# The Delta stage of a three-layer kernel: the first head's stage 1 and substitution go ahead of the second head's projections, and keys are projected first

## The chip, the core and the metric

The kernel runs on one core of one Trainium2 chip. The metric is the device time of one execution in microseconds (us). The core has five instruction queues that matter here: TensorE (PE, with its weight loads shown as PEld), VectorE (DVE), ScalarE (ACT), GpSimd (POOL) and SyncE (SP), which issues most DMA transfers.

## What is computed

The input is one sequence of 1024 positions with 1024 channels. Three layers follow each other: an RG-LRU block, a gated delta rule block with 8 heads of 128 channels, and a hybrid layer of a convolution and an S5 state space model. The change lies in the delta rule block alone. For one head, cut to what matters:

```python
q, k, v = silu(causal_dwconv(proj, conv_w))        # width 4, per channel
q, k = l2norm(q) * DK ** -0.5, l2norm(k)
a_mat = where(strict, einsum('cd,md->cm', k * beta, k) * decay_mask, 0)
t_mat = inverse(a_mat + eye)                       # per chunk, lower triangular
w, u = t_mat @ (k * beta * exp(g)), t_mat @ (v * beta)
for each chunk:                                    # the state S goes from chunk to chunk
    v_new = u - w @ S
    o = q_dec @ S + attn @ v_new
    S = S * e_last + k_dec.T @ v_new
```

The result of a head is normalised, gated with silu(z) and projected back to 1024 channels.

## The kernel before, in words

The kernel is one Python function in which every operation is given to a scheduler in program order, and the scheduler fixes each engine's list when the program is built. Program order is the priority: among the operations whose operands are ready by the scheduler's own estimate of durations, the one given earlier is placed first, and a later one fills a gap. On the chip every engine then runs its list in that fixed order and waits, with all that stands behind, where an operand is late. A tile of a pool has a tag and a number of buffers; a new tile waits until an old one of its tag is let go.

In the Delta stage (lines 608 to 959) the sequence is cut into 8 chunks (NT) of 128 positions. The gates of all heads are computed once (lines 614 to 654) and written to a DRAM tile `gb_d`. Then each of 8 heads (NH) goes through these helpers:

- `dense(h)` (line 677) projects q, k and v. On even heads it loads and splits three weight blocks, each good for two heads (`load_w`, lines 99 to 106: DMA into `wst`, ACT makes `wh`, DVE makes `wl`). Each of the three projections has two halves of 512 positions, each half 24 matmuls into one of three PSUM banks `psmm` (`mm_chT`, lines 108 to 113). ACT copies a half into `xp` (2 buffers, line 689), ACT and DVE apply the four convolution taps into `qT`, `kT` or `vT` (lines 691 to 694), and ACT applies SiLU (line 695). `qT` and `kT` have 3 buffers, `vT` has 1.
- `stage1(h)` (line 698) loads the head's gate row to all partitions into `GB` (1 buffer, SP, line 701), forms the decay `E` (DVE, line 705; ACT exponential, line 707) and its masked copy `U` (POOL, line 709). PE transposes k in the two PSUM banks of `ps_s` (`ps_tk`, line 722); ACT copies it and takes squares `jk` (line 726). PE multiplies k by k (`ps_kk`, line 735), DVE multiplies that into `U` (line 739), SP writes the diagonal blocks of `U` to DRAM in 4 transfers and reads them back as `Lp` in 4 (lines 745 and 747). Then follow the transposes of q and v and the product of q and k. `GB` is let go by line 772.
- `base(h)` (line 775) inverts the 32 by 32 diagonal blocks by substitution on DVE: 31 steps of a product `tm` and a difference `Tt` (lines 789 and 791), each waiting for the one before. SP writes the result in 4 transfers and reads it back as `TdT` in 4 (lines 793 and 795).
- `levels(h)` (line 797) joins the blocks to 64 and 128 with small matmuls; its first operation is a transpose on DVE (line 802).
- `chain(h)` (line 848) runs the 8 chunks one after another, PE, DVE and ACT in turn. It is the last user of the head's `qT` and `kT`.

`zgate(q)` (line 893) gates and transposes the outputs of two heads, and has projections of its own. The calls stand at lines 939 to 959: before, `dense(0)`, `dense(1)`, and then for each head `stage1(h)`, `base(h)`, `levels(h)`, `chain(h)` and `dense(h + 2)`. Since `dense(h + 2)` needs little of what comes before it, its matmuls serve as filling for PE while a chain waits. `ada_part` (line 172) and `ada_fin` (line 181) in heads 2 to 5 prepare the gate of the layer's residual.

Of the kernel before, what the change touches and what calls it, by code (L numbers as in the profile page):

```python
# [18 lines left out]
D = 1024  # L19
# [9 lines left out]
def kernel(ctx, tc, ins, out):  # L29
# [16 lines left out]
    def ps_mm(n="psmm"):  # L46
        return psmm.tile([P, 512], F32, tag="mm", name=n, bufs=3)

    def ps_c(n="psc"):
        return psmm.tile([P, 512], F32, tag="c", name=n, bufs=3)  # L50
# [48 lines left out]
    def load_w(src, c0, nk=NK, ncols=WC, pl=None, bufs=4):  # L99
        st = wstage().rearrange("p (k c) -> p k c", k=nk)[:, :, :ncols]  # L100
        sp.dma_start(st, src.rearrange("(k p) c -> p k c", p=P)[:, :, c0:c0 + ncols])
        hi = (pl or wpool).tile([P, nk, ncols], F16, tag="wh", name="wh", bufs=bufs)
        lo = (pl or wpool).tile([P, nk, ncols], F16, tag="wl", name="wl", bufs=bufs)
        act.activation(hi, st, AF.Copy, scale=WS)  # L104
        dve.scalar_tensor_tensor(out=lo, in0=st, scalar=WS, in1=hi, op0=ALU.mult, op1=ALU.subtract)  # L105
        return hi, lo

    def mm_chT(ps, w, c0, ah, al, nk=NK, ks=None):
        wh, wl = w
        for k in (range(nk) if ks is None else ks):  # L110
            pe.matmul(ps, wh[:, k, c0:c0 + P], ah(k), start=(k == 0), stop=False)  # L111
            pe.matmul(ps, wh[:, k, c0:c0 + P], al(k), start=False, stop=False)  # L112
            pe.matmul(ps, wl[:, k, c0:c0 + P], ah(k), start=False, stop=(k == nk - 1))  # L113
# [58 lines left out]
    def ada_part(pl, l, part, h, tag):  # L172
        acc = pl.tile([P, 512], F32, tag=tag, name="ad", bufs=2)
        for kk in range(2):
            st = wstage("wst_ada").rearrange("p (k c) -> p k c", k=4)
            sp.dma_start(st, ada_src(l, part, h, 4 * kk, 4))
            for k in range(4):
                ada_acc(acc, st[:, k, :], 4 * kk + k)
        return acc, l, part, h
# [48 lines left out]
    def col(nm, k, i=0):  # L228
        j = prow[nm] + i
        return cols[:, k, j:j + 1]  # L230
# [8 lines left out]
    def hTh(sl):  # L239
        t = hT["h"]  # L240
        return lambda k: t[:, k, sl]

    def hTl(sl):
        t = hT["l"]
        return lambda k: t[:, k, sl]
# [364 lines left out]
    with ExitStack() as s0:  # L610
# [65 lines left out]

        def dense(h):
            if h % 2 == 0:
                for nm, off in (("q", 0), ("k", D), ("v", 2 * D)):
                    wsets[nm] = load_w(in_w, off + P * h)  # L680
            for nm in ("q", "k", "v"):
                xp = pl.tile([P, T + 3], F32, tag="xp", name="xp", bufs=2)
                xt = (pl if nm == "q" else plA).tile([P, T], F32, tag=nm + "T", name=nm + "T", bufs={"q": 3, "k": 3, "v": 1}[nm])
                pool.memset(xp[:, 0:3], 0.0)
                for hf in range(2):
                    sl = slice(512 * hf, 512 * (hf + 1))
                    ps = ps_mm()
                    mm_chT(ps, wsets[nm], P * (h % 2), hTh(HF[hf]), hTl(HF[hf]))
                    act.activation(xp[:, 3 + 512 * hf:3 + 512 * (hf + 1)], ps, AF.Copy, scale=IWS)
                g = "g" + nm  # L690
                act.activation(xt, xp[:, 3:3 + T], AF.Copy, scale=col(g, h, 3))
                for i in range(3):
                    dve.scalar_tensor_tensor(out=xt, in0=xp[:, i:i + T], scalar=col(g, h, i), in1=xt,
                                             op0=ALU.mult, op1=ALU.add)
                act.activation(xt, xt, AF.Silu)
                qkv[nm, h] = xt
# [78 lines left out]
        def base(h):  # L775


            Lp = st_[h]["Lp"]
            tpd = tp_d[h % 2]
            Tt = gcol.tile([P, 8, 32], F32, tag="Tt", name="Tt")  # L780
            tm = gcol.tile([P, 8, 32], F32, tag="tm", name="tm")
            pool.tensor_copy(Tt, tinit)
            if h >= 2:

                pool.memset(TdTs[h % 2][0:32, :, 32:64], 0.0)
            for j in range(31):
                n, m = 31 - j, j // 4 + 1
                tv = tm[:, :m, :n]
                dve.tensor_tensor(out=tv, in0=Lp[:, j, j + 1:].unsqueeze(1).to_broadcast([P, m, n]),  # L789
                                  in1=Tt[:, :m, j:j + 1].to_broadcast([P, m, n]), op=ALU.mult)  # L790
                dve.tensor_tensor(out=Tt[:, :m, j + 1:], in0=Tt[:, :m, j + 1:], in1=tv, op=ALU.subtract)  # L791
            for q in range(4):
                sp.dma_start(tpd.rearrange("b c m i -> (b c) m i")[:, q::4, :], Tt[32 * q:32 * q + 32])
            for b in range(4):
                sp.dma_start(TdTs[h % 2][32 * b:32 * b + 32, :, 32 * b:32 * b + 32], tpd[b].rearrange("c m i -> m c i"))

        def levels(h):
            d = st_[h]
            U = d["U"]
            TdT = TdTs[h % 2]  # L800
            Td = pl.tile([P, NT, P], F32, tag="Td", name="Td")
            dve.transpose(Td.rearrange("p c t -> p (c t)"), TdT.rearrange("p c t -> p (c t)"))
            lo, hi = slice(0, 64), slice(64, 128)

            X = pl.tile([P, NT, 32], F32, tag="X", name="X")

            def v32(p):
                return p[:, :256].rearrange("p (c t) -> p c t", c=NT)

            blk = [(slice(r, r + 32), slice(r + 32, r + 64)) for r in (0, 64)]  # L810
            pxs = [v32(ps_c("ps_x")) for _ in blk]
            for c in range(NT):
                for (A, B), px in zip(blk, pxs):
                    pe.matmul(px[B, c, :], U[A, c, B], Td[A, c, A], start=True, stop=True)
            for n, ((A, B), px) in enumerate(zip(blk, pxs)):
                if n == 0:
                    act.activation(X[B], px[B], AF.Copy)
                else:
                    dve.tensor_copy(X[B], px[B])
            p1, p1t = v32(ps_c("ps_t1")), v32(ps_c("ps_t1t"))  # L820

            def t1(n, c):
                A, B = blk[n]
                pe.matmul(p1[B, c, :], TdT[B, c, B], X[B, c, :], start=True, stop=True)

            def t1t(n, c):
                A, B = blk[n]
                pe.matmul(p1t[A, c, :], X[B, c, :], TdT[B, c, B], start=True, stop=True)

            for n in range(2):  # L830
                for c in range(NT):
                    t1(n, c)
                    t1t(1 - n, c)
            for A, B in blk:
                dve.tensor_scalar(out=Td[B, :, A], in0=p1[B], scalar1=-1.0, scalar2=None, op0=ALU.mult)
                act.activation(TdT[A, :, B], p1t[A], AF.Copy, scale=-1.0)

            X2 = pl.tile([P, NT, 64], F32, tag="X2", name="X2")
            px = ps_c("ps_x2").rearrange("p (c t) -> p c t", c=NT)
            for c in range(NT):  # L840
                pe.matmul(px[hi, c, :], U[lo, c, hi], Td[lo, c, 0:64], start=True, stop=True)
            dve.tensor_copy(X2[hi], px[hi])
            px = ps_c("ps_t2t").rearrange("p (c t) -> p c t", c=NT)
            for c in range(NT):
                pe.matmul(px[lo, c, :], X2[hi, c, :], TdT[hi, c, hi], start=True, stop=True)
            dve.tensor_scalar(out=TdT[lo, :, hi], in0=px[lo], scalar1=-1.0, scalar2=None, op0=ALU.mult)
# [84 lines left out]
        def yload(q):  # L931
            if q < NH // 2 - 1:
                for e in range(2):
# [3 lines left out]
                    yT[2 * q + e] = yt  # L937

        dense(0)
        dense(1)  # L940
        adp = []
        for h in range(NH):

            if h in (2, 3):
                adp.append(ada_part(pl, 1, 2, h - 2, "zs"))
            elif h in (4, 5):
                ada_fin(pl, *adp.pop(0))
            stage1(h)
            base(h)
            levels(h)  # L950
            chain(h)
            if h + 2 < NH:
                dense(h + 2)
            if h == NH - 2:
                zgate(0)
# [596 lines left out]
```

## Time and profile before

| | us |
|---|---|
| median of 3 runs | 1832.92 |
| lowest and highest run | 1831.28, 1835.8 |
| the profiled execution | 1834.74 |
| its span in the profile | 1833.0 |
| PE, DVE, ACT busy in the span | 1751.7, 1380.0, 922.1 |

The profile shows one execution. Its times count from the start of the span; what lies outside of the span is the 1.74 us between the profiled execution's time and its span. "Busy" counts the union of an engine's instructions. Matmuls overlap, so that a matmul shown with 0.38 us may start 0.22 us after the one before. The note in brackets at the end of a timeline row is the engine's idle time just before it, and what ended it. The granted clock is the share of TensorE's full clock that it was given: 1.00 is the upper of its two levels (2.4 GHz), 0.50 the lower (1.2 GHz), and what lies between is a mean over a stretch.

### The profile page before, as it was taken

The page shows a single profiled execution, that of the slowest core. Times are in us where ns is not written, and L with a number is a line of the kernel's source. Part 1 is how long each engine was busy: PE and PEld are TensorE (multiplying, and loading weights), DVE is VectorE, ACT ScalarE, POOL GpSimd, SP SyncE. Part 2 cuts the span into 40 slices and gives each one's busy share as a digit, 9 for nine tenths or more (in the row PEclk, how much of TensorE's full clock was granted, in tenths as well). Part 3 has the DMA queues.
Part 4 walks back from the last instruction along what each step waited for, and adds up shares of the span by engine and source line. Part 5 has one row for each costly group of instructions (what it writes and reads, how often), then busy time and mean ns, then how long its engine had stood idle before and what let it go on. Part 6 is the DMA issues. An engine that isn't in the chain of part 4 may idle for free.

```text
span 1833.0 us, 29043 instructions
## 1 busy us (share of the span) xinstructions
PE 1751.7 (96%) x11623; PEld 1075.3 (59%) x11623; DVE 1380.0 (75%) x2408; ACT 922.1 (50%) x1644; POOL 60.8 (3%) x152
## 2 busy tenths in 40 slices
PE   4999899999899999999999998999999999999998
PEld 2444348955556656678789496555444444444487
DVE  6577776656787777887466799999999998693332
ACT  6577563256566857766444424655651221671221
POOL 0000000010000010100000300000000000000000
PEclk8999899999999999999999999999999999999999
DMA  9543425224132231344342311101321222011212
GB/s 307 161 157 92 103 71 185 88 75 129 33 118 70 62 79 33 113 130 121 123 150 82 88 50 52 53 20 50 127 80 35 71 67 68 25 46 47 81 70 92
DMA packets 165025, 165.23 MB, mean 90 GB/s; under 512 B 50078, under 2 KB 143326, under 8 KB 164890
## 3 DMA queue, kind: packets, MB, share of 16 engines
q1 hardware_dynamic: 163482, 159.17, 28.4%
q0 software_dynamic: 1408, 4.21, 0.6%
q8 instruction: 91, 1.49, 0.3%
q14 instruction: 44, 0.36, 0.1%
HBM read 139.05 MB, written 23.12 MB: 88 GB/s over the span
## 4 chain that ended last, share of the span: by engine, by line
PE 59%; DVE 26%; ACT 7%; issue 4%; DMA 3%; SPq 0%; DVEq 0%; ACTq 0%
DVE cc L1022 5%; PE psmm L111 4%; PE psmm L113 4%; PE psmm L112 4%; DVE wl L105 2%; PE ps_out L120 2%; PE ps_out L118 2%; PE ps_out L119 2%; PE ps_fin L118 2%; PE ps_fin L119 2%; PE ps_fin L120 2%; PE ps_zc L112 2%; PE ps_zc L111 2%; PE ps_zc L113 2%; ACT jk L726 1%
## 5 line engine op out<-in xcount | busy, mean ns | idle before, releaser
L111 PE MATMUL psmm<-hTh,wh 128*128 128x512 f16 x896 | 343.1, 384 | 2.5 <-ACT hTh L416 2.5
L113 PE MATMUL psmm<-hTh,wl 128*128 128x512 f16 x896 | 343.4, 383 | 0.0
L112 PE MATMUL psmm<-hTl,wh 128*128 128x512 f16 x896 | 343.3, 383 | 0.1
L1022 DVE SCALAR_TENSOR_TENSOR cc<-cu,cols,cc 128x1024 f32<-128x1024 f32 (+1 forms) x270 | 300.9, 1157 | 0.9
L113 PEld LDWEIGHTS <-wl 128*128 128x128 f16 x1568 | 154.4, 98 | 176.8 <-issue 11.0
L111 PEld LDWEIGHTS <-wh 128*128 128x128 f16 x1568 | 154.3, 98 | 175.7 <-issue 10.4
L112 PEld LDWEIGHTS <-wh 128*128 128x128 f16 x1568 | 154.4, 98 | 174.2 <-issue 9.9
L105 DVE SCALAR_TENSOR_TENSOR wl<-wst,wh 128x2048 f16<-128x2048 f32 (+2 forms) x71 | 153.5, 2166 | 56.9 <-ACT wh L104 56.8
L104 ACT ACTIVATE wh<-wst 128x2048 f16<-128x2048 f32 (+2 forms) x71 | 128.3, 1811 | 92.1 <-PE ps_gs L112 27.7
L118 PE MATMUL ps_z<-wh,hTh 128*128 128x256 f16 x256 | 69.8, 273 | 0.0
L119 PE MATMUL ps_z<-wh,hTl 128*128 128x256 f16 x256 | 69.8, 273 | 0.0
L120 PE MATMUL ps_z<-wl,hTh 128*128 128x256 f16 x256 | 69.8, 273 | 0.0
L118 PE MATMUL ps_fin<-wh,merged 128*128 128x256 f16 x256 | 69.8, 273 | 0.0
L119 PE MATMUL ps_fin<-wh,merged 128*128 128x256 f16 x256 | 69.8, 273 | 0.0
L120 PE MATMUL ps_fin<-wl,merged 128*128 128x256 f16 x256 | 69.8, 273 | 0.0
L118 PE MATMUL ps_out<-wh,hs 128*128 128x256 f16 x256 | 69.7, 273 | 0.0
L119 PE MATMUL ps_out<-wh,hs 128*128 128x256 f16 x256 | 69.7, 273 | 0.0
L120 PE MATMUL ps_out<-wl,hs 128*128 128x256 f16 x256 | 69.7, 273 | 0.0
L123 ACT ACTIVATE hTh<-ps_ht 128x512 f16<-128x512 f32 x32 | 17.4, 595 | 88.0 <-PE ps_ht L271 88.0
L791 DVE TENSOR_TENSOR Tt<-Tt,tm 128x60 f32<-128x60 f32 (+24 forms) x248 | 55.8, 225 | 5.5
L789 DVE TENSOR_TENSOR tm<-Lp,Tt 128x60 f32<-128x60 f32 (+24 forms) x248 | 53.4, 215 | 5.2
L120 PE MATMUL ps_out<-wl,yo 128*128 128x256 f16 x192 | 52.3, 273 | 0.3 <-DVE wl L105 0.3
(531 smaller groups left out, 4002.3 us busy)
## 6 DMA issues: line engine op xcount, KB each, us to landing
wst<-in_w_in_dram SPq DMA_DIRECT2D x24, 1024.0 KB
wst<-in_gdn_in_w_dram SPq DMA_DIRECT2D x16, 1024.0 KB
ast<-in_ada_w_dram SPq DMA_DIRECT2D x24, 512.0 KB
xt<-in_x_dram SPq DMA_DIRECT2D x16, 512.0 KB
wst<-in_lru_in_w_dram SPq DMA_DIRECT2D x8, 1024.0 KB
sta<-in_ada_w_dram SPq DMA_DIRECT2D x8, 1024.0 KB
wst<-in_lru_out_w_dram SPq DMA_DIRECT2D x4, 1024.0 KB
x_d<-xt POOLq DMA_DIRECT2D x8, 512.0 KB, 2.9
```

The source lines that it names most:

```text
L104: act.activation(hi, st, AF.Copy, scale=WS)
L105: dve.scalar_tensor_tensor(out=lo, in0=st, scalar=WS, in1=hi, op0=ALU.mult, op1=ALU.subtract)
L111: pe.matmul(ps, wh[:, k, c0:c0 + P], ah(k), start=(k == 0), stop=False)
L112: pe.matmul(ps, wh[:, k, c0:c0 + P], al(k), start=False, stop=False)
L113: pe.matmul(ps, wl[:, k, c0:c0 + P], ah(k), start=False, stop=(k == nk - 1))
L118: pe.matmul(ps, ah(k), wh[:, k, :], start=(k == 0), stop=False)
L119: pe.matmul(ps, al(k), wh[:, k, :], start=False, stop=False)
L120: pe.matmul(ps, ah(k), wl[:, k, :], start=False, stop=(k == nk - 1))
L726: act.activation(jk, pst[:, P * c:P * (c + 1)], AF.Square, accum_out=kq[:, n, 4 * b + c:4 * b + c + 1])
L789: dve.tensor_tensor(out=tv, in0=Lp[:, j, j + 1:].unsqueeze(1).to_broadcast([P, m, n]), in1=Tt[:, :m, j:j + 1].to_broadcast([P, m, n]), op= ...
L791: dve.tensor_tensor(out=Tt[:, :m, j + 1:], in0=Tt[:, :m, j + 1:], in1=tv, op=ALU.subtract)
L1022: dve.scalar_tensor_tensor(out=acc, in0=cus[j][:, i + t0:i + t0 + n], scalar=col("cw", j, i), in1=acc, op0=ALU.mult, op1=ALU.add)
```

## The change

In `dense`, the three weight blocks are loaded and the three projections are made in the order k, q, v instead of q, k, v, for every head. In the calls, `dense(1)` moves from before the loop into it: it is given after `stage1(0)` and `base(0)` and before `levels(0)`. Nothing else changes; the operations are the same in number and size.

```diff
@@ -676,9 +676,9 @@
         def dense(h):
             if h % 2 == 0:
-                for nm, off in (("q", 0), ("k", D), ("v", 2 * D)):
+                for nm, off in (("k", D), ("q", 0), ("v", 2 * D)):
                     wsets[nm] = load_w(in_w, off + P * h)
-            for nm in ("q", "k", "v"):
+            for nm in ("k", "q", "v"):
                 xp = pl.tile([P, T + 3], F32, tag="xp", name="xp", bufs=2)
@@ -937,7 +937,6 @@
         dense(0)
-        dense(1)
         adp = []
         for h in range(NH):
@@ -947,6 +946,8 @@
             stage1(h)
             base(h)
+            if h == 0:
+                dense(1)
             levels(h)
             chain(h)
             if h + 2 < NH:
```

## Rows read from the trace of the kernel before

**Rows 1.** The page, busy us of each engine (share of the span) and instructions.

```profile
PE 1751.7 (96%) x11623; PEld 1075.3 (59%) x11623; DVE 1380.0 (75%) x2408; ACT 922.1 (50%) x1644; POOL 60.8 (3%) x152
```

**Rows 2.** Stretches, Delta stage: from:to, length, busy by engine (instructions), clock, DMA share, GB/s.

```profile
480.00:500.00 20.00, 14.84 (x80) 9.94 (x82) 12.55 (x46) 13.26 (x48) 0.50 (x2) 0.83 0.23 46
...
640.00:660.00 20.00, 17.51 (x91) 10.03 (x90) 19.14 (x57) 13.41 (x33) 4.33 (x4) 0.91 0.41 73
...
760.00:830.00 70.00, 63.65 (x610) 52.75 (x608) 53.07 (x186) 47.45 (x146) 3.32 (x5) 1.00 0.39 117
...
370.00:920.00 550.00, 529.11 (x4244) 348.30 (x4243) 394.64 (x1111) 351.64 (x898) 28.75 (x53) 0.99 0.32 88
```

**Rows 3.** PE's waits, 360 to 960 us: waiting, releaser, total us, times, longest.

```profile
PE ps_kk L735 <- ACT jk L726: 7.8, 4, 5.5
PE ps_tk L722 <- DVE U L739: 3.7, 2, 1.9
...
PE ps_tv L762 <- ACT jk L726: 1.4, 6, 0.3
```

**Rows 4.** PE's timeline: start, duration, instruction, number, idle before and its releaser.

```profile
442.79 1.16 PE L735 MATMUL ps_kk<-kT 128*128 128x128 f32 x8
...
476.43 1.04 PE L722 MATMUL ps_tk<-ident,kT 128*128 128x128 f32 x8
...
484.88 2.08 PE L735 MATMUL ps_kk<-kT 128*128 128x128 f32 x8 [5.47 <-ACT jk L726]
...
487.61 1.87 PE L735 MATMUL ps_kk<-kT 128*128 128x128 f32 x8
```

**Rows 5.** ACT's timeline, heads 0 (384 to 408 us) and 2 (481 us).

```profile
384.51 0.60 ACT L689 ACTIVATE xp<-psmm 128x512 f32<-128x512 f32 x1 [2.97 <-PE psmm L113]
...
396.53 0.60 ACT L689 ACTIVATE xp<-psmm 128x512 f32<-128x512 f32 x1 [0.40 <-PE psmm L113]
...
406.92 1.06 ACT L707 ACTIVATE E<-E 128x1024 f32<-128x1024 f32 x1 [0.88 <-DVE E L705]
...
481.00 1.06 ACT L695 ACTIVATE kT<-kT 128x1024 f32<-128x1024 f32 x1 [6.07 <-DVE kT L693]
```

**Rows 6.** DVE's timeline, head 0's decay, multiplies, substitution and transpose.

```profile
405.23 1.66 DVE L705 TENSOR_SCALAR E<-GB,gc 128x128 f32<-128x128 f32 x8 [2.82 <-DMA GB<-gb_d]
...
445.38 2.16 DVE L739 SCALAR_TENSOR_TENSOR U<-ps_kk,Dc,U 128x128 f32<-128x128 f32 x8
...
461.71 0.18 DVE L789 TENSOR_TENSOR tm<-Lp,Tt 128x31 f32<-128x31 f32 x1
...
467.22 0.29 DVE L705 TENSOR_SCALAR E<-GB,gc 128x128 f32<-128x128 f32 x1 [4.01 <-DMA GB<-gb_d]
...
477.00 1.28 DVE L693 SCALAR_TENSOR_TENSOR kT<-xp,cols,kT 128x1024 f32<-128x1024 f32 x1
...
487.39 0.17 DVE L791 TENSOR_TENSOR Tt<-Tt,tm 128x8 f32<-128x8 f32 x1
...
498.54 1.24 DVE L802 STREAM_TRANSPOSE Td<-TdT 128x1024 f32<-128x1024 f32 x1
```

**Rows 7.** SP's timeline: issue of DMA transfers, start and time of the issuing.

```profile
397.60 0.37 SPq L701 DMA_DIRECT2D GB<-gb_d  x1
...
447.61 2.21 SPq L745 DMA_DIRECT2D lp_d<-U  x4
...
459.30 0.38 SPq L701 DMA_DIRECT2D GB<-gb_d  x1
...
487.60 2.61 SPq L793 DMA_DIRECT2D tp_d<-Tt  x4
```

**Rows 8.** A stretch in which PE only projects (columns of rows 2).

```profile
410.00:420.00 10.00, 10.00 (x48) 4.54 (x47) 4.88 (x4) 6.45 (x7) 0.39 (x2) 1.00 0.01 2
```

**Rows 9.** POOL's timeline, the mask of head 0.

```profile
408.05 1.09 POOL L709 TENSOR_SCALAR_AFFINE_SELECT U<-E 128x1024 f32<-128x1024 f32 x1 [5.39 <-ACT E L707]
```

## The prediction

> **What bounds the kernel now.** I read the page's busy times first, then stretches of the Delta stage, then PE's waits in it, and last the timelines of PE, ACT, DVE and SP around the longest wait. TensorE (PE) is busy for 96% of the span [rows 1], and the change neither adds nor removes a matmul. So it can only win or lose PE's idle time and the time at the lower clock, and, beyond what its own stage hands on, only inside the Delta stage. That stage runs from about 370 to 920 us. The reader should see in [rows 2] that PE is idle there for 550.00 - 529.11 = 20.9 us in all, in three places above all: 5.2 us at 480 to 500, 2.5 us at 640 to 660 and 6.4 us at 760 to 830. The first also has a granted clock of 0.83, the second 0.91. Nothing the change can do in this stage is worth much more than 20.9 us of idle time and some 4 us of lower clock.
>
> The largest wait of the stage is one of 5.5 us for `ps_kk`, released by ACT's squares `jk` [rows 3]. In PE's timeline [rows 4] it is the second head's stage 1: the transposes of k at 476.43, then nothing until 484.88, though projections of the third head stand behind it in PE's list. Its cause is followed backwards. ACT reached the squares late because a SiLU of the third head's k stood ahead of them and waited 6.07 us for DVE [rows 5]. DVE gave that k its taps only at 477.00, because the taps stood behind the first head's substitution; the substitution began at 461.71 and was held by 4.01 us, since the second head's `E` stood in DVE's list ahead of its second step and waited for `GB` [rows 6]. That `GB` load was issued only at 459.30 [rows 7], when stage 1 of the first head, put behind all of the second head's projections, let go of the single `GB` buffer. So the stall comes of a first head that is late: everything of head 0 that DVE does serially falls into the moment at which head 2's projections and head 1's stage 1 want DVE too.
>
> **The change, part by part.** *Second head's projections behind stage 1 and substitution of the first.* Instruction counts stay: 3 x 2 x 24 = 144 matmuls per head, at 48 in 10.00 us with PE full [rows 8] 30 us per head. What moves is the first head's stage 1 and substitution, with all that they issue: 1 load of `GB`, 4 writes and 4 loads for `Lp`, 4 writes and 4 loads for the inverse, all on SP's queue.
>
> When will head 0 be done? `GB` depends on the gates and not on the projections, so it lands as now: `E` starts at 405.23 [rows 6], the exponential ends at 406.92 + 1.06 = 407.98 [rows 5], the mask on POOL at 408.05 + 1.09 = 409.14 [rows 9], and the eight multiplies into `U` take 2.16 us [rows 6]: 411.3. From the writes of `U` at 447.61 [rows 7] to the first substitution step at 461.71 are 14.1 us, an upper bound as DVE was at other work: 425.4. The substitution took 461.71 to 487.56, 25.9 us; without the 4.0 us wait, three taps of 1.28 and eight `E` of 0.28 it is 15.7 us [rows 6]. That gives 441 to 451. From the writes at 487.60 [rows 7] to the transpose at 498.54 [rows 6] are 10.9 us: 452 to 462, against 498.54 now. The first head thus gets ready for its chain some 40 us earlier.
>
> What covers this? PE has the rest of head 0's projections to about 407 (second projection out at 396.53 [rows 5], 10 us for the third), then 30 us each of heads 1 and 2, to 467 without stage 1's own matmuls. The first head's waits are hidden by that, as long as they are not in front of it in PE's list. If this cover went, the 14.1 and 10.9 us round trips would lie bare. DVE's taps for head 1 now fall behind head 0's steps; two `xp` tiles and three PSUM banks hold 4 + 3 halves of 5 us, 35 us, more than the 25.9 us of the longest substitution shown, so I cost that at nothing. On SP, head 0's eight `Lp` transfers would stand ahead of the weights of heads 2 and 3, of which the first is needed only when head 1's projections end at about 437: nothing as well. On POOL only the two masks and the copy of `tinit` come earlier.
>
> *Stall removed.* With head 0's stage 1 done at about 415 the `GB` buffer is free some 40 us before head 1 wants it, and the substitution is over by 451, before head 2's k needs its taps. So the whole link breaks. It is worth the 5.47 us of wait [rows 4] and the clock: the kk matmuls took 2.08 and 1.87 us against 1.16 for the same eight at 442.79, 1.6 us, and some 0.4 us for the projections between them. Together 7.5 us.
>
> *Wait added.* Head 0 now passes stage 1 with PE waiting on it more closely. No row shows this pass. Below, its cost is 0: PE has projections to run. Above: the PSUM banks of its second transposes are held until the multiplies end at 411.3, and PE could come there when the second projection is out at 396.53: 14.8 us. The nearest rows are the waits that later heads pay in stage 1: 3.7 us for `U`, 7.8 - 5.5 = 2.3 for `jk` at kk and 1.4 at the v transposes [rows 3], over eight heads 0.9 us per head. I take 1.0. Queued behind such a wait on PE are head 1's projections, and ACT's copies out of PSUM wait for those.
>
> *Keys first.* Head 0's k is out at 384.51 where now q is, instead of 396.53 [rows 5], but its `U` waits for `GB` all the same. For later heads k is ready one projection (10 us) sooner, well ahead of stage 1. Nothing added; what it may save is in the rivals.
>
> **Sum**: -7.5 + 1.0 = -6.5 us. The profiled execution took 1834.74 us for a span of 1833.0; that becomes 1828.2. The median of the runs is 1832.92, and 6.5 less is 1826.4.
>
> **Rivals.** *The stall only moves.* Head 1's stage 1 is still behind head 2's projections in priority, and its squares still share ACT's fixed list with head 2's SiLUs. For it: the 2.5 us and 6.4 us idle at 640 to 660 and 760 to 830 [rows 2], where no first head is late. Against it: the `GB` load, the one transfer in the chain, does go early. Result -3 to +3, so about 1833.
>
> *Head 0's wait stands in PE's list (slower).* If the scheduler believes that `GB` lands sooner than it does, it places head 0's second transposes, or its v transposes, ahead of head 1's projections, and PE stands until 411.3. Price: up to 14.8 us and 2.0 us of lower clock as at 484.88, less the 7.5 removed: +9.3, 1842.2. For it: `GB` took 405.23 - 397.60 = 7.6 us and 467.22 - 459.30 = 7.9 us [rows 6, 7], and DVE idled before both [rows 6], so its list did expect them sooner. Against it: those two idled DVE by 2.82 and 4.01 us only, and PE not at all at the first. It decides once the new wait passes 11 us; if the old stall stays too, at 3.5 us. The rule behind it is in the Trainium skill, "TensorE: Matmul & The Clock Gate", step-by-step part: matmuls stay in program order, only weight loads are pulled ahead; the trace agrees, with 5.47 us in which ready projections were not started. The Trainium skill's page "DMA: Bandwidth & Descriptors", section on the anatomy of one DMA, gives 2.0 us plus bytes over 436 GB/s (fitted for the GpSimd path). For the 512 KB of `GB` that would be an estimated 3.2 us, this rival's worst case would end 4.4 us lower at about 1838, and the trace contradicts it with 7.6 and 7.9 us.
>
> *More goes than the first stall.* A first head 40 us ahead, and k a projection ahead, could take the waits of [rows 3] and the idle 2.5 and 6.4 us of [rows 2] as well: up to 7.5 + 2.5 + 6.4 = 16.4 us, 1816.5. Against it: DVE is busy 19.14 of 20.00 us at 640 to 660 [rows 2], and the change takes no work from it.
>
> **How the numbers follow.** A measurement of this kernel can tell about 0.3%, 5.5 us, so faster means under 1827.4 and slower over 1838.4. The forecast gets 0.46, with a spread of 3 us around 1826.4: 0.31 of it counts as faster, 0.15 as the same. The stall that moves gets 0.21, all same; the slower rival 0.18, of which 0.17 beyond 0.3%; the larger gain 0.15, all faster. That makes 0.46 faster, 0.37 same, 0.17 slower. I predict 1826.4 us. The range is 1817 to 1838: it reaches to the larger gain and over the moved stall, and leaves out the worse half of the slower rival.
>
> **What would show it.** Right: head 0's first substitution step near 425, its transpose at 452 to 462, a `GB` load of head 1 issued before 430, and a window 480 to 500 with PE above 19 us at clock 1.00. Wrong: a wait of several us for `ps_tk`, `ps_kk` or `ps_tv` between 395 and 415 (slower rival), a `jk` wait of 4 us or more in any head's stage 1 (moved stall), or a Delta stage ending at 920 as now with none of these, which would mean that PE was not what set its end.

## The result, and the profile after

The changed kernel is slower: 1848.61 us against 1834.36 us, medians of four runs each, a ratio of 1.0076 with a 95% interval of 1.0063 to 1.0089. The profiled execution took 1849.17 us for a span of 1847.5, against 1834.74 and 1833.0 before. That lies outside the range that was given; the forecast was 6.5 us faster, and the slower rival named the kind of loss but not its place or its size.

**Where the time is.** First the page's busy times of the changed kernel, to be held against [rows 1].

```profile
PE 1764.4 (96%) x11623; PEld 1086.0 (59%) x11623; DVE 1379.8 (75%) x2408; ACT 922.3 (50%) x1645; POOL 61.3 (3%) x152
```

PE has the same 11623 matmuls and is busy 12.7 us longer. So the matmuls themselves ran slower; that is the first sign that waiting alone is not the story. Next, stretches of the Delta stage of the changed kernel (columns as in [rows 2]).

```profile
400.00:420.00 20.00, 18.50 (x100) 9.95 (x99) 10.87 (x25) 16.47 (x42) 2.38 (x4) 1.00 0.10 24
...
460.00:480.00 20.00, 15.17 (x71) 6.64 (x69) 16.09 (x34) 7.41 (x9) 0.96 (x4) 1.00 0.35 93
480.00:500.00 20.00, 18.36 (x171) 12.89 (x171) 4.82 (x9) 5.21 (x17) 0.00 (x0) 0.57 0.01 2
500.00:540.00 40.00, 39.91 (x230) 24.20 (x229) 30.54 (x84) 32.09 (x87) 3.40 (x5) 1.00 0.25 70
540.00:560.00 20.00, 16.95 (x90) 10.21 (x89) 17.61 (x49) 12.73 (x41) 0.51 (x2) 0.91 0.57 169
640.00:660.00 20.00, 17.44 (x83) 8.68 (x83) 19.41 (x52) 13.67 (x22) 3.17 (x5) 0.95 0.48 137
720.00:740.00 20.00, 17.83 (x154) 14.48 (x153) 6.02 (x18) 7.57 (x35) 1.05 (x1) 0.66 0.12 30
760.00:830.00 70.00, 66.87 (x593) 51.06 (x591) 59.30 (x188) 47.14 (x125) 2.99 (x5) 1.00 0.41 122
370.00:960.00 590.00, 566.66 (x4459) 379.42 (x4457) 411.52 (x1134) 364.38 (x913) 29.26 (x53) 0.96 0.31 88
```

And those of the kernel before that [rows 2] does not have.

```profile
460.00:480.00 20.00, 19.41 (x94) 9.10 (x92) 15.20 (x48) 8.23 (x9) 2.33 (x3) 1.00 0.12 27
...
500.00:540.00 40.00, 37.44 (x310) 23.13 (x311) 33.45 (x90) 21.23 (x51) 0.40 (x2) 1.00 0.43 127
540.00:560.00 20.00, 19.21 (x131) 10.73 (x131) 13.28 (x36) 16.55 (x45) 2.84 (x5) 1.00 0.34 85
...
720.00:740.00 20.00, 19.91 (x128) 14.09 (x128) 12.71 (x32) 19.32 (x63) 0.10 (x1) 1.00 0.16 43
...
370.00:960.00 590.00, 567.77 (x4592) 382.37 (x4591) 423.49 (x1152) 370.96 (x925) 28.75 (x53) 0.99 0.33 93
```

What a stretch loses is its length less PE's busy time times the clock. PE's work is the same in both kernels, so the difference of the losses is the difference of the times.

| stretch, us | before loses | after loses |
|---|---|---|
| 400 to 420 | 0 | 1.50 |
| 460 to 480 | 0.59 | 4.83 |
| 480 to 500 | 20 - 14.84 x 0.83 = 7.68 | 20 - 18.36 x 0.57 = 9.53 |
| 500 to 540 | 2.56 | 0.09 |
| 540 to 560 | 0.79 | 20 - 16.95 x 0.91 = 4.58 |
| 640 to 660 | 4.07 | 3.43 |
| 720 to 740 | 0.09 | 20 - 17.83 x 0.66 = 8.23 |
| 760 to 830 | 6.35 | 3.13 |
| sum | 22.1 | 35.3 |

These stretches hold 13.2 of the 14.5 us. The reader should see one more thing: from 370 to 960 us PE is idle for 590 - 567.77 = 22.2 us before and 590 - 566.66 = 23.3 us after. The idle time has only moved. What grew is the time at the lower clock, in two places: 18.36 x 0.43 = 7.9 us at 480 to 500, where before it was 14.84 x 0.17 = 2.5, and 17.83 x 0.34 = 6.1 us at 720 to 740, where before it was nothing.

**The first place.** PE's waits after (columns as in [rows 3]; the first row is new, the jk wait has gone from 5.5 us to 2.5 at the longest, and from 7.8 to 6.1 in all).

```profile
PE ps_x L814 <- DVE Td L802: 6.5, 1, 6.5
PE ps_kk L735 <- ACT jk L726: 6.1, 4, 2.5
...
PE ps_t1t L828 <- issue: 2.2, 2, 1.9
...
PE ps_tk L722 <- DVE U L739: 0.8, 1, 0.8
```

PE's timeline at the first two of the new gaps (columns as in [rows 4]).

```profile
474.80 0.38 PE L111 MATMUL psmm<-hTh,wh 128*128 128x512 f16 x1
481.64 1.06 PE L814 MATMUL ps_x<-Td,U 32*32 32x32 f32 x32 [6.46 <-DVE Td L802]
482.63 0.61 PE L112 MATMUL psmm<-hTl,wh 128*128 128x512 f16 x1
...
723.17 0.24 PE L828 MATMUL ps_t1t<-TdT,X 32*32 32x32 f32 x1 [1.91 <-issue]
```

"A levels" is here and below one head's run of `levels`. At 474.80 PE has done all that its list puts ahead of head 0's levels, among it 274 projections of heads 1 and 2. The next projection, at 482.63, was ready (it goes on with the sum begun at 474.80) but stands behind `ps_x`, which wants Td. DVE's timeline says why Td is late, and SP's when the transfers went out.

```profile
432.89 0.18 DVE L789 TENSOR_TENSOR tm<-Lp,Tt 128x31 f32<-128x31 f32 x1
...
437.66 0.29 DVE L705 TENSOR_SCALAR E<-GB,gc 128x128 f32<-128x128 f32 x1 [3.26 <-DMA GB<-gb_d]
...
480.25 1.25 DVE L802 STREAM_TRANSPOSE Td<-TdT 128x1024 f32<-128x1024 f32 x1 [1.58 <-DMA TdT<-tp_d]
```

```profile
428.33 0.38 SPq L701 DMA_DIRECT2D GB<-gb_d  x1
...
472.84 2.61 SPq L793 DMA_DIRECT2D tp_d<-Tt  x4
```

Behind the gap the clock is at its lower level, in stretches of 5 us (columns as in [rows 2]); the last three are the second place.

```profile
485.00:490.00 5.00, 5.00 (x60) 3.20 (x58) 1.53 (x3) 0.75 (x2) 0.00 (x0) 0.50 0.00 0
490.00:495.00 5.00, 5.00 (x25) 3.07 (x24) 0.70 (x2) 0.00 (x0) 0.00 (x0) 0.50 0.01 3
495.00:500.00 5.00, 5.00 (x30) 4.13 (x27) 0.92 (x3) 4.08 (x14) 0.00 (x0) 0.74 0.01 2
500.00:505.00 5.00, 5.00 (x38) 4.08 (x36) 2.07 (x9) 4.19 (x22) 0.00 (x0) 1.00 0.00 0
...
725.00:730.00 5.00, 5.00 (x31) 4.00 (x30) 2.15 (x8) 0.72 (x4) 0.00 (x0) 0.50 0.01 3
730.00:735.00 5.00, 5.00 (x28) 4.18 (x27) 2.07 (x6) 0.23 (x1) 0.00 (x0) 0.50 0.00 0
735.00:740.00 5.00, 5.00 (x32) 3.99 (x31) 0.99 (x3) 4.30 (x21) 0.00 (x0) 0.85 0.47 117
```

PE is busy without a break there, at 0.50 of its clock, 1.2 instead of 2.4 GHz. What it runs are the levels, 32x32 and 64x64 matmuls (481.6 to 493.0 us, and 718.6 to 731.5 us for head 4), with ten projections among them for head 0, and some projections and kk matmuls for head 4.

### The profile page after: what moved, and what is told of

Read it like the earlier page. It is cut to its first block, busy times and chain, and to the rows that moved or that the text cites. A ratio compares the mean times of both kernels' runs of the same rounds, so it can differ in the third digit from the quotient of the medians.

```text
span 1847.5 us, 29051 instructions
## 1 busy us (share of the span) xinstructions
PE 1764.4 (96%) x11623; PEld 1086.0 (59%) x11623; DVE 1379.8 (75%) x2408; ACT 922.3 (50%) x1645; POOL 61.3 (3%) x152
## 4 chain that ended last, share of the span: by engine, by line
PE 56%; DVE 28%; ACT 7%; issue 4%; DMA 3%; SPq 0%; DVEq 0%; ACTq 0%
DVE cc L1023 5%; PE psmm L113 4%; PE psmm L112 4%; PE psmm L111 4%; DVE wl L105 3%; PE ps_out L120 2%; PE ps_out L118 2%; PE ps_out L119 2%; PE ps_fin L120 2%; PE ps_fin L118 2%; PE ps_fin L119 2%; PE ps_zc L113 1%; PE ps_zc L112 1%; PE ps_zc L111 1%; DVE kT L693 1%
```

## The experiments

The first theory was that the move alone makes the loss, by the first place, and that the second place follows from it. The base of each edit is named; "moved" means `dense(1)` ahead of `levels(0)` as in the changed kernel.

**Keys first alone** (from before; the weight loads alike):

```diff
-            for nm in ("q", "k", "v"):
+            for nm in ("k", "q", "v"):
```

> Keys projected first in each head, and the second head's projections at their old place ahead of the first head's stage 1. Theory 1 (the move alone costs the time: it puts head 0's levels into PE's list at a place where their input Td is late): as before, 1829 to 1840 us, the ps_kk wait of about 5.5 us near 480 us and the granted clock of 0.8 at 480 to 500 as before, no wait of ps_x for Td above 2 us. Theory 2 (the new order of the projections costs the time, by shifting how the later heads' steps meet): 1843 us or more, with a stretch at clock 0.5 to 0.7 near 720 to 740 us.

Measured: 1838.0 us, ratio 1.0021 (1.0010 to 1.0031). The wait near 480 stays (5.2 us). As theory 1 had it; keys first alone costs 0.2%.

**The move alone** (from the changed kernel; the weight loads alike):

```diff
-            for nm in ("k", "q", "v"):
+            for nm in ("q", "k", "v"):
```

> Second head's projections moved as in the changed kernel, queries still first. Theory 1 (the move alone costs the time): as the changed kernel, 1844 to 1853 us, with a wait of PE at ps_x for head 0's Td of 5 to 8 us near 475 to 485 us, the clock at 0.5 to 0.6 for some 15 us behind it, and the last gate's first SiLU about 14 us later than the 920.0 us of before. Theory 2 (the order of the projections costs it): 1838 us or less, and head 0's levels without a wait above 3 us.

Measured: 1838.59 us, ratio 1.0014 (1.0002 to 1.0027). The profile shows the first place in full, and no second one:

```profile
PE ps_x L814 <- DVE Td L802: 6.5, 1, 6.5
```

```profile
480.00:500.00 20.00, 19.43 (x180) 13.48 (x180) 4.42 (x10) 6.51 (x24) 0.00 (x0) 0.61 0.01 2
...
720.00:740.00 20.00, 19.98 (x146) 14.25 (x146) 10.93 (x27) 16.27 (x55) 2.18 (x2) 1.00 0.14 34
```

Each theory holds in half: the wait and the clock of theory 1 and, within 0.6 us, the time of theory 2. Against before, 0.14% is lost, so the first place costs little more than the move saves elsewhere; the changed kernel's 14 us need the second place, and that needs keys first as well. Theory 1 falls.

**One substitution step in head 0** (from the changed kernel; 30 of head 0's 31 steps are left out):

```diff
-            for j in range(31):
+            for j in range(1 if h == 0 else 31):
```

> The changed kernel with only 1 of the 31 substitution steps in head 0 (30 steps of head 0 are left out; the other heads are whole). Theory 1 (late Td, then the clock): Td of head 0 comes about 25 us or more earlier, so no wait at ps_x in head 0, no stretch at clock 0.5 to 0.6 near 480 to 500 us, PE above 19 us of 20 there; the 6.5 us wait and about 8 us of low clock go, 14 us together: 1832 to 1837 us if the dip near 720 us stays, about 8 us less if that one follows from the first. Rival (the clock falls because the levels are 32x32 and 64x64 matmuls with few projections between, wait or no wait): the clock is at 0.5 to 0.6 for 10 us or more at head 0's levels also here, wherever they fall, and the time stays above 1838 us.

Measured: 1846.76 us, ratio 1.0067 (1.0053 to 1.0081). Td is early and 480 to 500 is clean, as theory 1 had it, but the gap has only gone to 445 to 451 us, and the time is the rival's. SP's transfers of the result, DVE's transpose and PE's wait:

```profile
430.48 2.96 SPq L793 DMA_DIRECT2D tp_d<-Tt  x4
440.75 0.38 SPq L176 DMA_DIRECT2D wst_ada<-in_ada_w_dram  x1
441.32 1.84 SPq L795 DMA_DIRECT2D TdT<-tp_d  x4
```

```profile
449.70 1.24 DVE L802 STREAM_TRANSPOSE Td<-TdT 128x1024 f32<-128x1024 f32 x1
```

```profile
451.08 1.07 PE L814 MATMUL ps_x<-Td,U 32*32 32x32 f32 x32 [6.18 <-DVE Td L802]
```

Td is 30 us earlier and the wait is as long as ever, since the scheduler puts the levels sooner too: 152 projections stand ahead of them instead of 274. So the length of the substitution is not what makes the wait. PE's list has the levels at a place where Td is not there yet; here the way from `tp_d` to Td took 19.2 us, against 7.4 in the changed kernel. Of the 11.8 us more, some 4 passed on SP, where the reads of `tp_d` stood behind a load of the residual's weights that went out only at 440.75, once DVE had let go of its buffer; some 3 on DVE, where the transpose stood behind pieces of the residual's gate and taps of q; and some 5 in the transfers themselves. The rival's cause does not hold either: head 0's levels, with 28 projections among them, lost 1.8 us of clock. A kk wait of 6.6 us and one of 2.5 us in head 4's levels make up the rest.

**Head 0's levels later** (from the changed kernel):

```diff
             if h == 0:
                 dense(1)
+                stage1(1)
+                base(1)
             levels(h)
```

(and no second call of both for head 1)

> The changed kernel, with stage 1 and substitution of head 1 also ahead of head 0's levels and chain in the source, so that head 1's stage 1 stands ahead of head 0's levels in PE's list; nothing is left out. Theory 1 (head 0's levels stand in PE's list before Td is there): the levels of head 0 find Td ready or wait less than 3 us, no clock below 0.9 at 470 to 500 us, and the first head's part of the loss (6.5 us of wait and 8 us of clock) goes: 1830 to 1840 us. Rival (DVE is what is short, and every head's wait only moves): another wait of 4 us or more for a DVE result takes its place at head 0's levels or at stage 1 of head 1 or 2, time 1842 to 1855 us.

Measured: 1858.99 us, ratio 1.0132 (1.0111 to 1.0152), the slowest of all. Head 0's levels wait for nothing and run at full clock, as theory 1 had it, yet other waits take over: 5.6 us at kk (twice), 3.2 us and 1.7 us at or in the levels of heads 4 and 3, with 8.3 and 5.1 us of clock behind them.

From here on **theory 3** was tested: the sum of PE's waits hardly changes, and what costs is the clock where a gap falls on a levels.

**Keys first in heads 0 to 3, moved** (from the changed kernel; the weight loads alike):

```diff
-            for nm in ("k", "q", "v"):
+            for nm in (("k", "q", "v") if h < 4 else ("q", "k", "v")):
```

> Second head's projections moved as in the changed kernel, keys first only in heads 0 to 3, queries first in heads 4 to 7. Theory 3 (the sum of PE's waits hardly changes; what the changed kernel loses is the clock, which stays low where a gap in PE is followed by the levels' small matmuls; the second such place, near 720 us, comes from the order of the projections in the later heads, which shifts what PE does around head 4's levels): no gap above 1 us in head 4's levels, clock above 0.95 at 715 to 740 us, the first place (wait of 6.5 us for Td, then clock about 0.53 for some 18 us) as in the changed kernel, time as with the move alone, 1834 to 1842 us. Rival (keys first in the first heads, which the change is about, sets the second place off): a gap of some 2 us near 720 us and 6 us of lower clock, 1845 to 1851 us.

Measured: 1837.86 us, ratio 1.0012 (1.0002 to 1.0022); in the profile, 720 to 740 is at full clock and has no gap. The profiled execution, 1833.71 us, lies 4 us under the median of the runs, so what the others did there was not seen; the median is as theory 3 had it.

**Third head's projections ahead too** (from the move alone):

```diff
                 dense(1)
+                dense(2)
             levels(h)
```

(and no second call for head 2)

> Second head's projections moved, queries first, and the third head's projections also given ahead of head 0's levels, so that 14 more projections (3 us at 48 in 10 us) stand ahead of head 0's levels in PE's list. Theory 3: the wait of ps_x for Td falls from 6.5 to about 3.5 us, and the clock is still low through all of head 0's levels, 6 to 8 us of loss, so about 3 us less than with the move alone: 1832 to 1838 us if no other gap falls on a levels. Rival (the clock's loss follows the length of the wait): the loss at head 0's levels halves to about 4 us, 1828 to 1834 us. Second rival (DVE's lateness only moves): another wait of 3 us or more in stage 1 of head 1, time as with the move alone or more.

Measured: 1838.59 us, ratio 1.0017 (1.0006 to 1.0027). The wait fell to 3.5 us and the clock's loss behind it stayed at 6.8 us, as theory 3 had it, so the loss does not follow the length of the wait. The time did not fall; 540 to 560 lost 5.5 us where the move alone lost 4.3, with a kk wait of 3.8 us, as the second rival had it in kind.

**The gap ahead of wide matmuls** (from the changed kernel; the results of the extra ones are not used; a line in `base` that hands on `Tt` is left out here):

```diff
+            if h == 0:
+                psw = ps_c("ps_w")
+                for i in range(14):
+                    pe.matmul(psw[:, :256], ident, d["Tt"].rearrange("p m i -> p (m i)"), start=True, stop=True)
```

> The changed kernel with 14 extra matmuls (128x256, results unused) that read head 0's substitution result Tt; in PE's list they stand 15 projections ahead of head 0's levels, so the gap falls ahead of wide matmuls and not ahead of the levels. Theory 3: PE waits several us for Tt near 465 to 473 us, the clock is low for some 4 to 8 us only (1.5 to 3 us lost, not 8), head 0's levels start with a wait below 2 us and run at 1.0 in 7 to 9 us instead of 11.4. The extra matmuls cost up to 6 us themselves, so 1838 to 1847 us. Rival (the levels' small matmuls lower the clock by themselves): clock about 0.5 through head 0's levels here too, 1846 us or more.

Measured: 1848.6 us, ratio 1.0070 (1.0058 to 1.0082), above the time expected. The clock came as theory 3 had it. The wait, and the stretches behind it (the levels are the second):

```profile
PE ps_w L814 <- DVE Tt L791: 8.5, 1, 8.5
```

```profile
470.00:480.00 10.00, 6.59 (x22) 5.57 (x23) 3.13 (x8) 1.06 (x1) 0.10 (x1) 0.66 0.16 25
...
486.00:495.00 9.00, 9.00 (x149) 5.63 (x147) 5.83 (x7) 3.34 (x6) 0.10 (x1) 1.00 0.01 2
```

A longer gap than the changed kernel's, 8.5 us, costs 1.8 us of clock, and head 0's levels run at 1.00. What follows the gap decides. The second place is gone too, though heads 4 to 7 have the order of the changed kernel:

```profile
720.00:740.00 20.00, 19.83 (x220) 12.80 (x219) 13.16 (x35) 14.88 (x38) 3.15 (x5) 1.00 0.09 13
```

The 6.2 us of clock won at the first place (8.0 over the whole low stretch, less 1.8) and the 6.5 at the second are given back by the extra matmuls, busy for 8.1 us, and by PE's idle time in the stage, 28.5 us instead of 23.3.

**The kernel before with a late Td** (from before, ahead of the writes of `tp_d`):

```diff
+            if h == 0:
+                for _ in range(1):
+                    sp.dma_start(tx_d, Tt)
+                    sp.dma_start(Tt, tx_d)
```

(the line that makes `tx_d`, a tile in DRAM, is left out)

> The kernel before, with the result of head 0's substitution sent once more to DRAM and back, so that Td comes some 4 to 8 us later; in PE's list head 0's levels move back by 14 projections (3 us). Theory 3: PE stands 1 to 5 us at ps_x for Td near 500 to 508 us, and if it stands 2 us or more the levels of head 0 run at clock about 0.5 for 10 us or more, 5 to 8 us lost beside the gap, time 1841 to 1850 us. Rival (a gap costs its length and some 1.6 us of clock wherever it falls): 1835 to 1840 us.

Measured: 1825.26 us, ratio 0.9947 (0.9935 to 0.9959): faster, where neither theory had it. Td comes 4.3 us later, and the levels stand 14 projections later in the list, so that PE does not wait for it; idle time falls all over the stage. Which of the changes in the list does that is not shown.

```profile
500.00:540.00 40.00, 40.00 (x331) 24.31 (x330) 35.39 (x97) 23.16 (x58) 0.40 (x2) 1.00 0.50 146
...
640.00:660.00 20.00, 19.43 (x107) 10.75 (x106) 15.87 (x49) 15.58 (x44) 3.22 (x5) 1.00 0.37 59
...
370.00:960.00 590.00, 575.26 (x4655) 387.69 (x4653) 424.63 (x1158) 369.71 (x927) 28.30 (x56) 0.99 0.34 96
```

PE is idle for 14.7 us there instead of 22.2. Theory 3's idle time that only moves holds for the changed kernel, not for every list.

**Keys first in heads 4 to 7, moved** (from the changed kernel; the weight loads alike):

```diff
-            for nm in ("k", "q", "v"):
+            for nm in (("k", "q", "v") if h >= 4 else ("q", "k", "v")):
```

> Second head's projections moved, keys first only in heads 4 to 7 (queries first in heads 0 to 3). Theory 3 (the order of the later heads' projections, not that of the first heads, places the second stretch of low clock): as the changed kernel, 1845 to 1851 us, with a gap of about 2 us in head 4's levels near 720 us and 6 us or more of clock loss behind it; beside the wait of 6.5 us for head 0's Td. Rival (it takes keys first in all heads, or the second place comes and goes by chance): 1834 to 1842 us, no gap there.

Measured: 1848.1 us, ratio 1.0066 (1.0043 to 1.0088). The second place is back:

```profile
PE ps_t1t L828 <- issue: 2.1, 1, 2.1
```

```profile
720.00:740.00 20.00, 18.89 (x115) 15.03 (x115) 7.21 (x23) 8.81 (x37) 0.00 (x0) 0.74 0.14 34
```

With the run of heads 0 to 3 this settles it: the 10 us between the move alone and the changed kernel come from the order of the projections in the later heads, some 240 us behind the moved step.

**The changed kernel with a late Td** (the edit of the kernel before, on the changed one):

> The changed kernel with the extra round trip of head 0's substitution result that made the kernel before faster in the run before last. Td comes about 4.3 us later (measured there: 498.54 to 502.81), PE's list has 15 more projections and 8 transposes (4 us) ahead of head 0's levels. Theory 3 (the gain there came of a list in which levels stand later than Td, not of the round trip): the gap before head 0's levels stays 5 to 8 us, the levels run at about 0.5 for 10 us or more, 6 to 8 us of clock lost, time not below 1836 us. Rival (the round trip as such helps): 8 to 10 us less than the changed kernel, 1838 to 1841 us, with less idle time in the stage by 7 us, as there.

Measured: 1851.26 us, ratio 1.0076 (1.0051 to 1.0101). A gap of 6.0 us, 7.2 us of clock behind it, and two more levels with gaps of 1.0 and 1.1 us and 5 us of clock each. Theory 3 holds; the round trip as such does not help.

**The kernel before with a late Td and keys first:**

> The kernel before with the extra round trip, and keys first in each head; the second head's projections at their old place. Theory 3: no wait above 1 us ahead of any head's levels, clock loss in the stage below 8 us, 1822 to 1831 us. Rival (keys first costs time by itself, as 0.2% in the run alone): 1830 us or more, with a gap on a later head's levels.

Measured: 1827.46 us, ratio 0.9952 (0.9934 to 0.9970). Idle 16.8 us, clock loss 3.9 us. Theory 3's numbers, but for a wait of 1.3 us ahead of a levels, which lowered no clock.

**Head 1's stage 1 ahead of head 0's levels** (from before):

```diff
+            if h == 0:
+                stage1(1)
             levels(h)
```

(and no second call for head 1)

> The kernel before (queries first, second head's projections at their old place) with stage 1 of head 1 given ahead of head 0's levels; nothing added. In PE's list head 0's levels stand 15 projections (3 us) later, as with the extra round trip, and head 1's transposes of k some 90 projections (19 us) sooner. Theory 3 (PE's idle time comes of list places that are earlier than their data): Td of head 0 is there when its levels come up, no gap of 2 us ahead of any levels, the ps_kk wait of 5.5 us near 480 us is gone, 1820 to 1832 us. Rival (DVE and ACT set the pace, so the wait only moves): idle time in the stage of 20 us or more, with a new wait of 3 us or more for U, jk or GB in head 1, 1832 to 1842 us.

Measured: 1847.94 us, ratio 1.0060 (1.0037 to 1.0084). The rival was right and more: the wait moved to 5.9 us for U, and a wait of 3.7 us ahead of head 4's levels took 8.1 us of clock with it.

**64 and 128 more matmuls at the start.** What still lacked a cause was the 2 us gap in head 4's levels.

```diff
+    psi = ps_c("ps_i")
+    for _ in range(64):
+        pe.matmul(psi[:32, :32], ident[:32, :32], ident[:32, :32], start=True, stop=True)
```

> The changed kernel with 64 extra 32x32 matmuls (results unused) as PE's first work, in the first 11 us, where PE has nothing to do; every engine's list is otherwise the same. Theory 4 (the gap of about 2 us in head 4's levels, for which the profile names no releaser, hangs on where in PE's stream of instructions those 128 tiny instructions lie, since the stream is loaded in blocks): the gap near 720 us is gone or below 1 us, with it the 6 us of clock loss behind it, while the wait of 6.5 us for head 0's Td and its 8 us of clock loss stay: 1838 to 1843 us. Rival (it hangs on what the list has there, on data or on another engine): the gap stays at 2 to 2.7 us, 1846 to 1851 us.

> The same with 128 extra matmuls, so 256 more instructions with their weight loads, which at 16 KB to one load of the instruction queue is an estimated whole block if an instruction has 64 bytes. Theory 4 with that block: the gap near 720 us is back as in the changed kernel, about 2 us and 6 us of clock loss, 1846 to 1851 us. Theory 4 with another block length: gone or moved, 1836 to 1843 us. Rival (hangs on the list): as the changed kernel, and so is the run with 64.

Measured: 1849.09 us, ratio 1.0081 (1.0052 to 1.0109), and 1843.97 us, ratio 1.0053 (1.0029 to 1.0077). In both profiles the gap is there:

```profile
PE ps_t L827 <- issue: 2.7, 1, 2.7
```

```profile
PE ps_t L827 <- issue: 2.6, 1, 2.6
```

It comes after 56 and 57 of the 64 small matmuls, after 58 of them in the changed kernel. So it hangs on what the list has there, and theory 4 falls. The seven runs with 128 lie at 1843 to 1844 (four) and 1848 to 1853 (three, the profiled one among them); whether the lower ones have the gap was not seen.

Which part of the list makes it stays open, but one thing in the traces goes with it. POOL issues two transfers of 2 KB in the stage, for the residual's gate; this is the second in the changed kernel:

```profile
715.11 0.77 POOL L189 DMA_DIRECT2D ada_d<-adac  x1 [0.35 <-issue]
```

Its landing is recorded at 720.92 and 720.93, then at 723.24 to 723.52, on either side of the gap from 721.26 to 723.17, and the trace has 5 of its 16 landing records. The same goes for all five kernels that have such a gap (the fourth is the one with keys first in heads 4 to 7, the fifth the one with head 0's levels later, where the gap of 1.7 us is in head 3's levels and the transfer is the first): landings are recorded just ahead of the gap and again within 0.3 us of its end, with 2 to 5 records of 16. In the kernel with one step the landing begins at the very end of the 64 matmuls, also with 5 of 16, and there DVE stands behind them, and PE behind DVE:

```profile
724.33 0.88 DVE L835 TENSOR_SCALAR Td<-ps_t 32x256 f32<-32x256 f32 x2 [3.54 <-remote]
```

In the other ten kernels neither transfer lands on a run of these 64. That the landing is the cause was not tested.

## Why the prediction was wrong, step by step

**Stall removed, -7.5 us: right where it was looked for.** The kk wait near 480 is gone; with its clock that stretch had lost 7.68 us. (PE did not stand from the transposes at 476.43 on, as the text has it: nine projections ran first, to 479.41.) `GB` of head 1 went out at 428.33, before 430 as foretold. 2.5 us at 500 to 540 and 3.2 us at 760 to 830 went too, the latter as the rival of the larger gain had it. Part of the wait came back, as the moved stall had it: 540 to 560 lost 3.8 us more, with a kk wait of 2.5 us.

**Wait added in stage 1, +1.0 us: right in size**, 1.50 us at 400 to 420, for kk.

**The cover of head 0's path, costed at nothing: the step that failed first.** The text said that the first head's waits are hidden "as long as they are not in front of it in PE's list", and put the transpose at 452 to 462 and the substitution at 25.9 us for the longest. It came at 480.25. The first step came at 432.89 instead of near 425, since `U` was written at 418.54 and not at 411.3, with head 0's v taps ahead of it on DVE. Then the steps took 40 us, since DVE's list held head 1's `E` with its 3.26 us wait, taps and weight splits between them. Lateness alone need not cost: with the levels later in the list PE did not wait for Td. The condition was the point, and it was weighed at stage 1 only: head 0's levels stand in PE's list after 274 projections of later heads, and with Td late PE waits 6.46 us with projections ready behind. The rule cited from the Trainium skill, "TensorE: Matmul & The Clock Gate", step-by-step part, that matmuls stay in program order, was the right one, applied to the wrong wait. The one-step run shows that the wait does not go with the length of the substitution: with Td 30 us earlier it was 6.18 us, since the levels moved up in the list and other work stood ahead of Td on SP and DVE. Of the four signs named for being right only the `GB` load came.

**The clock, 2.0 us a gap: mis-sized.** That price came from a gap followed by kk and projections [rows 4]. Behind a gap that falls on the levels it was 8.0 and 6.5 us in the changed kernel. Over the 16 kernels, from 440 us on, taking as low each stretch of 1 us with a granted clock under 0.9 (it can begin within the gap):

| the gap in PE falls | stretches | at low clock, us | lost, us |
|---|---|---|---|
| ahead of or in a levels, 1 us or more | 17 of 20 | 11 to 22 | 5.0 to 8.3 |
| the same, in the kernel with one step in head 0 | 2 of 20 | 7 and 8 | 3.1 and 1.8 |
| the same, in the kernel before with a late Td and keys first | 1 of 20 | none | 0 |
| ahead of transposes, kk, projections or other wide work, where the clock fell | 31 | 4 to 11 | 1.4 to 3.1 |

A gap need not lower the clock: before, 2.56 us at 521.27 cost none (500 to 540 at 1.00 in the row above).

**Keys first, "nothing added": the second failed step.** Alone it costs 0.2%; with the move, in heads 4 to 7, it costs 10 us (1837.86 against 1848.1), by a gap in head 4's levels whose cause is open, and the clock behind it. Nothing in the profile of before shows that place; what could have been seen is that every head's order changes the list, not only that of the first two.

**The slower rival** had the mechanism, a wait in PE's order, at a place that cost 1.5 us, and its price of 9.3 us lacked the clock behind the levels. **The sum by what was measured**, from the table: -7.7 + 9.5 + 4.2 at 460 to 500, -2.5 at 500 to 540, +3.8 at 540 to 560, -0.6 at 640 to 660, +8.1 at 720 to 740, -3.2 at 760 to 830, +1.5 at 400 to 420: some 13 of the 14.5 us.

## What to carry to other kernels

Moving work in program order changes an in-order list everywhere, so for each moved step look for the first instruction on the busiest engine that waits for it, and for what stands behind that. Price a gap by what follows it: ahead of wide matmuls it cost its length and up to 3 us of clock, ahead of a run of small ones, in 17 of 20 cases, its length and 5 to 8 us. Where an engine's idle time moves from place to place with every variant, judge a variant by idle time and clock loss summed over the stage, and expect edits that look neutral to be worth several us either way; the two versions that beat both kernels here did it with an extra transfer, with which the list placed head 0's levels later.

## What the runs showed of the hardware

- With PE busy without a break, the clock stayed at 0.50 to the end of the levels and came back 2.5 to 5.2 us later in 16 of the 17 cases of the table's first row (in the changed kernel levels until 493.0, full clock from 497.6; until 731.5, from 736.5); in one it came back 0.8 us ahead of the end. The 108 levels that met no gap of 1 us ran at full clock, in 6.2 to 9.4 us. The Trainium skill, "TensorE: Matmul & The Clock Gate", section on the clock gate, calls the warm-up a budget of time and not a number of matmuls; these traces do not show one such time, with 4 to 11 us at the lower clock where wide work followed a gap and 11 to 22 us where a levels did.
- PE stood for 1.7 to 2.7 us inside a run of 64 small matmuls, after 56 to 62 of them, with no releaser in the profile, in five of the 16 kernels. In these five a small transfer of POOL's landed around that moment, and in ten of the others it landed on no such run. The cause is open.
- From the issue of head 0's writes to the last landing of the reads back it took 7.2 us in the changed kernel and 16.2 us with one step, with the same transfers; 4 us of the second are SP's, behind another load. Td came 0.2 and 3 us after that.
